# Trunk of a two-layer diffusion backbone: the first modulations by quarters of the features, one multiply for each value, and a new order of the start

## The chip, the cores and the metric

The kernel runs on one core of a Trainium2 chip. The metric is the time of one execution in microseconds (us), as the device measures it; the median of the runs is compared. The engines are PE (TensorE: matrix products; PEld is its weight load), DVE (VectorE), ACT (ScalarE), POOL (GpSimd) and SP (SyncE, which here only issues DMA loads). Each works through its own list of instructions, in the order of the code.

## The reference

Two layers over 256 latent tokens of 1024 features, with 256 context tokens ahead of the first. What the change touches is the head of layer 0:

```python
sh1, sc1, g1, sh2, sc2, g2 = jnp.split((c_s @ ada_w[i] + ada_b[i])[:, None, :], 6, axis=-1)
h = rmsnorm(x, norm1_g[i]) * (1 + sc1) + sh1
csh1, csc1, cg1, csh2, csc2, cg2 = jnp.split(cc_s @ ada_w[i] + ada_b[i], 6)
hc = rmsnorm(ctx, norm1_g[i]) * (1 + csc1) + csh1
q, k, v, f = jnp.split(h @ w_in, [DIFF_QK, 2 * DIFF_QK, 2 * DIFF_QK + DIFF_V], axis=-1)
kc, vc = jnp.split(hc @ w_in[:, DIFF_QK:2 * DIFF_QK + DIFF_V], [DIFF_QK], axis=-1)
```

`c_s` and `cc_s` are silu of the conditioning vectors of the tokens and of the context. After this come the attention with its six heads, a Fourier mixer, an output projection, an expert network with 16384 experts, a second layer of another kind with its own expert network, and a last norm.

## The kernel before

Features lie on partitions, tokens along the free axis: `x` and `xc` (context) are eight tiles of 128 features by 256 tokens. Products are made in fp32 out of parts: a value is split into a high part (a rounded copy, ACT) and a low part (the difference, DVE), and three products stand for one. Weights come in units of 128 x 1024 values (512 KB) through `Stream`: SP loads a unit into one of four buffers `raw`; `_split` makes `whi` on ACT (L109) and `wlo` on DVE (L111); the next load that gets the buffer waits until the split is done. Loads are issued in one order, so one that waits holds up those behind it.

The start of layer 0 is written out by hand in the string `START`; its words are run one after another, and each engine gets its instructions in that order:

- `M0` to `M15`: the 16 units of `ada_w` for shift and scale, a product of 2 or 4 rows with 512 columns each (`modulation`). M0 to M7 are used raw, in fp32 products (L547); M8 to M15 are split first (L555). Four units make one row of 512 columns.
- `sc`/`sx`, `ic`/`ix`, `rc`/`rx`: sum of squares, its inverse root (`ir`: DVE L269, then POOL L270), and its spread over all partitions (PE L277, ACT copy `rstd`), for context and for x.
- `C0`, `C1`: `columns` copies finished rows to SBUF (`ar`), turns them on PE into columns (L565), and makes shift `sh` and scale `sc` of a half of the features (L570 to L573).
- `nc0` to `nx7`: one normalisation each, on DVE (L596).
- `Dc0`, `Dx0`, `Dc1`, `Dx1`: `modulate`, for context (c) or x, a half of the features: scale and shift (ACT, `h`, L602), high part (ACT, L603: `chi` of context, `thi` of x) and low part (DVE, L604: `clo`, `tlo`).
- `Q` with three digits: a part of the value projection, of column chunk 0 to 2, token block 0 to 3 (0 and 1 context, 2 and 3 x) and half of the features: 12 products of 128 x 256 (L248 to L250). All chunks together are 288 products.
- `S`: split weights ahead; `a`: one step of another modulation, which DVE sums by itself (L445); `V`: the finished values leave PSUM.

The first product of the next part, the keys of head 0, is the first row `mm<-thi,whi` of L241. From there the six heads follow, with an order string of their own.

Of the kernel before, what the change touches and what calls it, by code (L numbers as in the profile page):

```python
# [20 lines left out]
P = 128  # L21
D = 1024
KT = 8
# [25 lines left out]
HL_BUFS = 3  # L49
MIX_BUFS = 6  # L50
# [7 lines left out]
START = "Lc Lx M0 sc M1 M2 M3 M4 M5 sx ic ix b S M6 S rc nc2 nc1 nc0 rx nc6 nx1 nx2 nc3 M7 nx0 nx3 C0 S nx4 M8 S Dc0 M9 S Dx0 Q000 M10 nx5 S Q010 M11 nc4 M12 Q020 nx7 S nc5 M13 Q030 M14 nc7 M15 nx6 C1 Q100 S Lk Q110 Dx1 Dc1 a Q120 S Q021 Q130 Q121 Q001 S Q101 Q111 a S Q031 a a Q011 V0 Q131 a Q220 S Q200 a a Q230 Q210 Q221 a S Q201 V1 a S Q231 S Q211 a V2".split()  # L58
# [5 lines left out]
class Stream:  # L64
# [4 lines left out]
    def __init__(self, nc, raw_pool, hl_pool):  # L69
        self.nc = nc  # L70
        self.raw_pool, self.hl_pools = raw_pool, [hl_pool, None]
# [16 lines left out]
    def load(self):  # L88
        while self.loaded < len(self.specs) and self.loaded < self.freed + RAW_BUFS:
            t = self.raw_pool.tile([P, 1024], F32, name="raw")  # L90
            self.nc.sync.dma_start(t, self.specs[self.loaded][0])
            self.raw[self.loaded] = t
            self.loaded += 1
# [49 lines left out]

    def next(self):
# [7 lines left out]
        self.cur = self.specs[n][2]  # L152
# [11 lines left out]
def trunk(ctx, tc, a, out):  # L164
# [344 lines left out]
    with ExitStack() as mx:  # L509
# [14 lines left out]
        with tc.tile_pool(name="m0n", bufs=2) as npl:  # L524
# [11 lines left out]
            rows = {}  # L536
# [57 lines left out]
            def normalize(j, k):  # L594
                dst, src, r = ((xn, x, st.get("x")), (xc, xc, st.get("c")))[j]
# [898 lines left out]
```

## Time and profile before

| | |
|---|---|
| median of 3 runs | 1973.15 us (1973.15 to 1973.7) |
| the profiled execution | 1970.44 us, of which its span 1968.7 |
| PE busy, share of the span | 98% |
| DVE, ACT busy | 80%, 48% |
| granted clock of PE, mean | 0.994 |
| from start to the first value product / the first key product | 30.09 / 77.67 us |

The profiled execution is one run; its times are taken from the span's first instruction. PE's busy share counts modelled ends of pipelined products, so a busy PE is not a PE at its peak. The granted clock is a share of 2.4 GHz.

### The profile page before, as it was taken

The numbers are of one execution on the slowest core, as the hardware profiler recorded it, in microseconds if no ns is written. First come the engines' busy times: TensorE is split into PE (matmuls) and PEld (weight loads), VectorE is DVE, ScalarE is ACT, GpSimd is POOL, SyncE is SP. The second block draws the span as 40 slices with busy tenths as digits, with TensorE's granted clock in tenths as the row PEclk, the third lists the DMA queues.
The fourth block names the chain that finished last, engine by engine and source line by source line (L and its number), as shares of the span: only waits on it lengthen the run. The fifth ranks groups of instructions, "written<-read, shape, count | busy, mean of one in ns | idle before, by whom it ended". The sixth has DMA issues, their size and how long they took to land. (4 is left out here: it accounts for less than half of the span.)

```text
span 1968.7 us, 35611 instructions
## 1 busy us (share of the span) xinstructions
PE 1924.6 (98%) x14172; PEld 1723.6 (88%) x14172; DVE 1567.0 (80%) x2972; ACT 939.1 (48%) x1493; POOL 11.6 (1%) x18
## 2 busy tenths in 40 slices
PE   7999999999999999999999899999999999999998
PEld 3977999999999877788888899999999987778886
DVE  5786779987887899998888678997777788885555
ACT  5445554444444444444445554445444444444544
POOL 0000000000000000000000000000000000000000
PEclk9999999999999999999999999999999999999999
DMA  7742556665666566678885365655555555556563
GB/s 266 266 165 82 159 175 185 186 184 188 199 184 185 186 208 206 210 253 284 280 280 186 132 186 172 187 184 183 171 165 168 169 169 173 165 173 196 178 191 119
DMA packets 106295, 374.03 MB, mean 190 GB/s; under 512 B 11920, under 2 KB 12560, under 8 KB 105744
## 3 DMA queue, kind: packets, MB, share of 16 engines
q1 hardware_dynamic: 104256, 366.23, 58.9%
q10 hardware_dynamic: 1872, 5.53, 0.9%
q8 instruction: 111, 1.82, 0.4%
q14 instruction: 56, 0.46, 0.1%
HBM read 370.66 MB, written 1.05 MB: 189 GB/s over the span
## 5 line engine op out<-in xcount | busy, mean ns | idle before, releaser
L111 DVE TENSOR_TENSOR wlo<-raw,whi 128x1024 fp32r<-128x1024 f32 x604 | 736.9, 1222 | 276.6 <-ACT whi L109 262.8
L109 ACT ACTIVATE whi<-raw 128x1024 fp32r<-128x1024 f32 x604 | 636.0, 1055 | 395.7 <-PE acc L1159 319.1
L241 PE MATMUL acc<-thi,whi 128*128 128x256 f32 (+1 forms) x2016 | 572.3, 285 | 0.0
L241 PE MATMUL acc<-thi,wlo 128*128 128x256 f32 (+1 forms) x2016 | 568.8, 283 | 0.4 <-DVE wlo L111 0.4
L241 PE MATMUL acc<-tlo,whi 128*128 128x256 f32 (+1 forms) x2016 | 559.8, 281 | 0.0
L241 PEld LDWEIGHTS acc<-thi,wlo 128*128 128x128 f32 x2016 | 382.9, 190 | 1.0 <-DVE wlo L111 0.8
L241 PEld LDWEIGHTS acc<-thi,whi 128*128 128x128 f32 x2016 | 382.1, 190 | 0.0
L241 PEld LDWEIGHTS acc<-tlo,whi 128*128 128x128 f32 x2016 | 376.4, 188 | 0.0
L1159 PE MATMUL acc<-whi,thi 128*128 128x512 f32 x1024 | 287.2, 400 | 0.0
L1159 PE MATMUL acc<-whi,tlo 128*128 128x512 f32 x1024 | 282.5, 396 | 0.2 <-DVE tlo L497 0.2
L1159 PE MATMUL acc<-wlo,thi 128*128 128x512 f32 x1024 | 282.2, 395 | 0.0
L1180 ACT ACTIVATE A<-acc 128x256 f32<-128x256 f32 x240 | 92.6, 386 | 391.5 <-PE acc L241 391.5
L1159 PEld LDWEIGHTS acc<-wlo,thi 128*128 128x128 f32 x1024 | 192.6, 188 | 47.5
L1159 PEld LDWEIGHTS acc<-whi,tlo 128*128 128x128 f32 x1024 | 192.6, 188 | 45.5 <-DVE tlo L497 0.6
L1159 PEld LDWEIGHTS acc<-whi,thi 128*128 128x128 f32 x1024 | 186.8, 188 | 38.9
L241 PE MATMUL mm<-thi,whi 128*128 128x256 f32 (+1 forms) x448 | 128.7, 287 | 0.9 <-ACT qp L1094 0.9
L241 PE MATMUL mm<-tlo,whi 128*128 128x256 f32 (+1 forms) x448 | 127.1, 284 | 2.4 <-DVE tlo L352 2.4
L241 PE MATMUL mm<-thi,wlo 128*128 128x256 f32 (+1 forms) x448 | 126.5, 282 | 0.0
L497 DVE TENSOR_TENSOR tlo<-A,thi 128x256 fp32r<-128x256 f32 x256 | 106.8, 418 | 0.0
L1144 DVE SCALAR_TENSOR_TENSOR A<-gg,A 128x512 f32<-128x512 f32 x128 | 87.6, 684 | 20.4 <-PE gg L1141 20.3
L496 ACT ACTIVATE thi<-A 128x256 fp32r<-128x256 f32 x256 | 102.5, 401 | 0.0
L1130 DVE TENSOR_TENSOR og<-o,gT 128x512 f16<-128x512 f16 x256 | 96.4, 417 | 0.1
(269 smaller groups left out, 1976.8 us busy)
## 6 DMA issues: line engine op xcount, KB each, us to landing
raw<-in_eu SPq DMA_DIRECT2D x256, 512.0 KB, 3.6
raw<-in_ev SPq DMA_DIRECT2D x256, 512.0 KB, 4.2
raw<-in_ada1t SPq DMA_DIRECT2D x56, 512.0 KB, 4.4
raw<-in_wq SPq DMA_DIRECT2D x32, 512.0 KB, 4.2
ada<-in_ada0t SPq DMA_DIRECT2D x48, 256.0 KB, 4.8
raw<-in_ada0h SPq DMA_DIRECT2D x16, 512.0 KB, 4.5
raw<-in_w_out SPq DMA_DIRECT2D x16, 512.0 KB, 3.7
raw<-in_o_in_u SPq DMA_DIRECT2D x8, 512.0 KB, 4.8
```

The source lines that it names most:

```text
L109: nc.scalar.activation(hi, r, AF.Copy)
L111: nc.vector.tensor_tensor(lo, r, hi.bitcast(F32), op=OP.subtract)
L241: nc.tensor.matmul(o, lhsT=w[:, k, :], rhs=t[:, k, :n], start=first and j == 0 and i == passes[0], stop=last and j == len(order) - 1 and i ...
L496: A_.activation(hi, src, AF.Copy)
L497: V.tensor_tensor(lo, src, hi.bitcast(F32), op=OP.subtract)
L1130: V.tensor_tensor(og[j], o1, of(gT[j], t0, 64), op=OP.mult)
L1144: return lambda: V.scalar_tensor_tensor(av, pt.rearrange("p t i -> p i t"), 1.0 / GSCALE, av, op0=OP.mult, op1=OP.mult)
L1159: nc.tensor.matmul(y[2 * h + tt], lhsT=w[a_][:, tt * P:tt * P + P], rhs=e[b_][:, 512 * h:512 * h + 512], start=i == 0 and n == 0, stop=i = ...
L1180: A_.activation(A[i // 64][:, i % 64, :], p[:, :T], AF.Gelu_apprx_tanh)
```

## The change

The rows of `ada_w` are laid out anew: a row of 512 columns is now shift and scale of one quarter of the features (two tiles of 128), so that four units give all that a quarter needs. `columns` is split in two: `A` copies the row (`row_out`), `C` turns it, with four products in place of eight transposes; for split rows a small matrix `pair` adds the two parts in the same product. There is no normalisation any more: `modulate` multiplies value, scale and inverse root in one DVE instruction (`t`, L613), ACT adds the shift and rounds (L615), and DVE makes the low part from `t` and the shift (L616). `Q`'s last digit now counts quarters, so that a `Q` has 6 products. The split units M8 to M15 have three buffers of their own. `S` is now exactly one split (`one`), and the words of `START` stand in a new order, in which context's quarter is modulated and multiplied while the units of later quarters are still to come. `START` holds 8 words `a` where it held 10; the heads take the steps that are left.

```diff
+ADA_BUFS = 3
...
-START = "Lc Lx M0 sc M1 M2 M3 M4 M5 sx ic ix b S M6 S rc nc2 nc1 nc0 rx nc6 nx1 nx2 nc3 M7 nx0 nx3 C0 S nx4 M8 S Dc0 M9 S Dx0 Q000 M10 nx5 S Q010 M11 nc4 M12 Q020 nx7 S nc5 M13 Q030 M14 nc7 M15 nx6 C1 Q100 S Lk Q110 Dx1 Dc1 a Q120 S Q021 Q130 Q121 Q001 S Q101 Q111 a S Q031 a a Q011 V0 Q131 a Q220 S Q200 a a Q230 Q210 Q221 a S Q201 V1 a S Q231 S Q211 a V2".split()
+START = "l1 Lc l4 M0 Lx b sc M1 M2 ic S M3 A0 rc C0 Dc0 Q000 Q010 M4 S Q100 Q110 sx M5 S ix M6 S rx Dx0 Q020 Q030 M7 A1 S Q120 Q130 M8 C1 Dc1 S Q001 Q011 M9 S Q101 Q111 Dx1 M10 S Q021 Q031 M11 A2 S Q121 Q131 S C2 Dc2 Q002 Q012 M12 S Q102 Q112 Dx2 M13 S Q022 Q032 M14 M15 A3 S Q122 Q132 C3 Dc3 Q003 Q013 Lk Q103 Q113 Dx3 Q023 Q033 S Q123 V0 Q133 a V1 Q200 Q210 a Q220 Q230 a Q201 Q211 S Q221 Q231 a Q202 S Q212 Q222 Q232 a a Q203 Q213 Q223 a Q233 a V2".split()
...
-    def load(self):
-        while self.loaded < len(self.specs) and self.loaded < self.freed + RAW_BUFS:
+    def load(self, n=RAW_BUFS):
+        while self.loaded < len(self.specs) and self.loaded < self.freed + n:
...
+    def one(self):
+
+        while self.specs[self.next_split][1] == "raw":
+            self.next_split += 1
+        n = self.next_split
+        self.load()
...
+        self._split(n)
+        self.next_split += 1
...
-            S.add(a["ada0h"][n:], 1, "raw" if n < 8 else "split")
-        if s[0] == "Q" and s[1::2] not in seen:
-            seen.add(s[1::2])
-            S.add(a["w_in_v"][2 * int(s[1]) + int(s[3]):], 1, "split")
+            S.add(a["ada0h"][n:], 1, "raw" if n < 8 else "split", 2 * (n >= 8))
+        if s[0] == "Q" and (s[1], int(s[3]) // 2) not in seen:
+            seen.add((s[1], int(s[3]) // 2))
+            S.add(a["w_in_v"][2 * int(s[1]) + int(s[3]) // 2:], 1, "split")
...
+    A_.dma_start(cols, a["cols"])
...
+    A_.dma_start(ident, a["consts"][:, K_ID:K_FOLD])
...
-            A_.dma_start(cols, a["cols"])
-            S.load()
-            A_.dma_start(ident, a["consts"][:, K_ID:K_FOLD])
-            sh = npl.tile([P, KT, 2], F32, name="sh", bufs=1)
-            sc = npl.tile([P, KT, 2], F32, name="sc", bufs=1)
+            ss = npl.tile([P, 2, KT, 2], F32, name="ss", bufs=1)
+            sh, sc = ss[:, 0], ss[:, 1]
             b2 = npl.tile([P, 16, 2], F32, name="b2", bufs=1)
-            xn = npl.tile([P, KT, T], F32, name="xn", bufs=1)
+            pair = npl.tile([4, 2], F32, name="pair", bufs=1)
...
-            def columns(half):
-                w = 2 + 2 * half
-                ar = npl.tile([4, 1024], F32, name="ar", bufs=1)
-                A_.activation(ar[:w, 0:512], rows[2 * half][0:w, :], AF.Copy)
-                A_.activation(ar[:w, 512:1024], rows[2 * half + 1][0:w, :], AF.Copy)
+            def row_out(c):
+                w = 2 if c < 2 else 4
+                ars[c] = npl.tile([4, 512], F32, name="ar")
+                A_.activation(ars[c][:w], rows.pop(c)[0:w, :], AF.Copy)
+
+            def columns(c):
+
+                w = 2 if c < 2 else 4
+                ar = ars.pop(c)
                 p = gb()
-                for n in range(8):
-                    nc.tensor.transpose(p[:, w * n:w * n + w], ar[:w, n * P:(n + 1) * P], ident[0:w, 0:w])
-                pv = p[:, :8 * w].rearrange("p (s c m) -> p s c m", s=2, m=w)
-                k = slice(4 * half, 4 * half + 4)
-                bias = b2.rearrange("p (s c) m -> p s c m", s=2)[:, :, k]
-                for i, o in enumerate((sh, sc)):
-                    V.tensor_tensor(o[:, k], pv[:, i, :, 0:2], bias[:, i], op=OP.add)
-                    if half:
-                        V.tensor_tensor(o[:, k], pv[:, i, :, 2:4], o[:, k], op=OP.add)
+                for n in range(4):
+                    nc.tensor.matmul(p[:, 2 * n:2 * n + 2], lhsT=ar[:w, n * P:(n + 1) * P],
+                                     rhs=ident[0:2, 0:2] if w == 2 else pair, start=True, stop=True)
+                k = slice(2 * c, 2 * c + 2)
+                V.tensor_tensor(ss[:, :, k], p[:, :8].rearrange("p (s c m) -> p s c m", s=2, m=2),
+                                b2.rearrange("p (s c) m -> p s c m", s=2)[:, :, k], op=OP.add)
                 V.scalar_tensor_tensor(sc[:, k], sc[:, k], 1.0,
-                                       ncol(C_NORM + 4 * half, 4)[:, :, None].to_broadcast([P, 4, 2]),
+                                       ncol(C_NORM + 2 * c, 2)[:, :, None].to_broadcast([P, 2, 2]),
                                        op0=OP.add, op1=OP.mult)
 
             def square_sums(src):
@@ -591,17 +606,14 @@
                 A_.activation(t, spread(r), AF.Copy)
                 return t
 
-            def normalize(j, k):
-                dst, src, r = ((xn, x, st.get("x")), (xc, xc, st.get("c")))[j]
-                V.tensor_tensor(dst[:, k, :], src[:, k, :], r, op=OP.mult)
-
-            def modulate(half, js):
-                for j, src, hi, lo in (((0, xn, thi, tlo), (1, xc, chi, clo))[js],):
-                    for k in range(4 * half, 4 * half + 4):
-                        h = npl.tile([P, T], F32, name="h", bufs=4)
-                        A_.activation(h, src[:, k, :], AF.Identity, scale=sc[:, k, j:j + 1], bias=sh[:, k, j:j + 1])
-                        A_.activation(hi[:, k, :T], h, AF.Copy)
-                        V.tensor_tensor(lo[:, k, :T], h, hi[:, k, :T].bitcast(F32), op=OP.subtract)
+            def modulate(c, j):
+                src, r, hi, lo = ((x, st.get("x"), thi, tlo), (xc, st.get("c"), chi, clo))[j]
+                for k in range(2 * c, 2 * c + 2):
+                    t = npl.tile([P, T], F32, name="t", bufs=4)
+                    V.scalar_tensor_tensor(t, src[:, k, :], sc[:, k, j:j + 1], r, op0=OP.mult, op1=OP.mult)
+                    b = sh[:, k, j:j + 1]
+                    A_.activation(hi[:, k, :T], t, AF.Identity, bias=b)
+                    V.scalar_tensor_tensor(lo[:, k, :T], t, b, hi[:, k, :T].bitcast(F32), op0=OP.add, op1=OP.subtract)
...
-            def quarter(outs, part, i, half):
-                for k in range(4 * half, 4 * half + 4):
+            def quarter(outs, part, i, c):
+                for k in range(2 * c, 2 * c + 2):
                     wide_part(outs[i], part, acts[i], k, k == 0 and i % 2 == 0, k == KT - 1 and i % 2 == 1)
...
                 elif c == "S":
-                    S.ahead()
+                    S.one()
+                elif c == "l":
+                    S.load(int(n))
...
                     V.tensor_copy(b2, ncol(C_ADAB, 16)[:, :, None].to_broadcast([P, 16, 2]))
+                    V.tensor_tensor(pair, ident[0:4, 0:2], ident[0:4, 2:4], op=OP.add)
...
-    w = f["ada_w"][0][:, :2048].reshape(4, 2, P, 2, 2, 512)
-    a["ada0h"] = np.ascontiguousarray(w.transpose(4, 3, 0, 2, 1, 5)).reshape(16, P, 1024)
+    w = f["ada_w"][0][:, :2048].reshape(4, 2, P, 2, 4, 256)
+    a["ada0h"] = np.ascontiguousarray(w.transpose(4, 0, 2, 1, 3, 5)).reshape(16, P, 1024)
```

How the order moves, at three places. PE, the beginning of the program (`mm<-raw,cs` are M units, `gg<-ones,sq` sums of squares, `gg<-ident,ir` the spread, `gg<-ident,ar` the turn). Before:

```order
L547 MATMUL mm<-raw,cs 2x512 x12
L264 MATMUL gg<-ones,sq 128x1 x4
L547 MATMUL mm<-raw,cs 2x512 x2
L277 MATMUL gg<-ident,ir 128x128 x4
L547 MATMUL mm<-raw,cs 2x512 x2
L565 MATMUL gg<-ident,ar 128x2 x8
L555 MATMUL mm<-whi,csr 4x512
```

and now:

```order
L561 MATMUL mm<-raw,cs 2x512 x6
L280 MATMUL gg<-ones,sq 128x1 x2
L561 MATMUL mm<-raw,cs 2x512 x2
L293 MATMUL gg<-ident,ir 128x128 x2
L583 MATMUL gg<-ident,ar 128x2 x4
L264 MATMUL acc<-whi,chi 128x256
```

The first value product (`acc<-whi,chi`) stands behind four M units and not behind ten; the sums and the spread of x have gone further down.

DVE, around the inverse roots (`raw_150` and `raw_154` are M8 and M9). Before:

```order
L269 TENSOR_SCALAR ir_164<-gg_161 128x2
L269 TENSOR_SCALAR ir_170<-gg_167 128x2
L648 COPY b2_118<-cols_71 128x32
L111 TENSOR_TENSOR wlo_175<-raw_150,whi_174 128x1024
L111 TENSOR_TENSOR wlo_179<-raw_154,whi_178 128x1024
```

and now, from the second value unit on (`raw_145`; `raw_208` and `raw_231` are M8 and M9, `ir_240` is x's):

```order
L112 TENSOR_TENSOR wlo_205<-raw_145,whi_204 128x1024
L596 TENSOR_TENSOR sq_224<-sq_224 128x1024
L596 TENSOR_TENSOR sq_224<-sq_224 128x512
L596 TENSOR_TENSOR sq_224<-sq_224 128x256
L112 TENSOR_TENSOR wlo_234<-raw_208,whi_233 128x1024
L285 TENSOR_SCALAR ir_240<-gg_237 128x2
L112 TENSOR_TENSOR wlo_248<-raw_231,whi_247 128x1024
L613 SCALAR_TENSOR_TENSOR t_256<-x_73,ss_111,rstd_251 128x256
L616 SCALAR_TENSOR_TENSOR tlo_85<-t_256,ss_111,thi_84 128x256
L613 SCALAR_TENSOR_TENSOR t_260<-x_73,ss_111,rstd_251 128x256
L616 SCALAR_TENSOR_TENSOR tlo_85<-t_260,ss_111,thi_84 128x256
```

The inverse root of x has moved from ahead of all splits to behind M8's, and the modulation is a chain that goes through ACT between each `t` and its low part.

ACT and DVE at the third quarter (`ar_398` is its row, `raw_290` a value unit, `raw_328` M13, `ss` shift and scale). ACT now:

```order
L575 ACTIVATE ar_398<-mm_304 4x512
L110 ACTIVATE whi_400<-raw_290 128x1024
L110 ACTIVATE whi_418<-raw_328 128x1024
L615 ACTIVATE chi_91<-t_431,ss_111 128x256
L615 ACTIVATE chi_91<-t_435,ss_111 128x256
```

DVE now:

```order
L112 TENSOR_TENSOR wlo_401<-raw_290,whi_400 128x1024
L112 TENSOR_TENSOR wlo_419<-raw_328,whi_418 128x1024
L586 TENSOR_TENSOR ss_111<-gg_424,b2_112 128x2x4
L588 SCALAR_TENSOR_TENSOR ss_111<-ss_111,cols_71 128x4
L613 SCALAR_TENSOR_TENSOR t_431<-xc_110,ss_111,rstd_165 128x256
```

and DVE before, at the second half's columns (`raw_305` is M15, `raw_311` a value unit):

```order
L111 TENSOR_TENSOR wlo_383<-raw_305,whi_382 128x1024
L111 TENSOR_TENSOR wlo_389<-raw_311,whi_388 128x1024
L596 TENSOR_TENSOR xn_119<-x_72,rstd_194 128x256
L570 TENSOR_TENSOR sh_116<-gg_402,b2_118 128x8
```

Two splits stand ahead of the scale in both, but before there was one such place, now there are three, the one after C3 with one split ahead.

## Rows read from the trace of the kernel before

**Rows 1.** The page, part 1: busy us of each engine (share of the span).

```profile
PE 1924.6 (98%) x14172; PEld 1723.6 (88%) x14172; DVE 1567.0 (80%) x2972; ACT 939.1 (48%) x1493; POOL 11.6 (1%) x18
```

**Rows 2.** Timeline of PE: start us, us, engine, line, operation [idle before <-releaser].

```profile
5.21 9.58 PE L547 MATMUL mm<-raw,cs 128*2 128x512 f32 x16 [5.21 <-ACT cs L233]
...
19.89 1.88 PE L547 MATMUL mm<-raw,cs 128*2 128x512 f32 x4
...
26.20 0.40 PE L555 MATMUL mm<-whi,csr 128*4 128x512 f32 x1
...
27.83 0.39 PE L555 MATMUL mm<-wlo,csr 128*4 128x512 f32 x1
30.09 0.38 PE L248 MATMUL acc<-whi,chi 128*128 128x256 f32 x1 [1.87 <-ACT chi L603]
...
50.10 0.28 PE L249 MATMUL acc<-wlo,chi 128*128 128x256 f32 x1
50.22 0.28 PE L250 MATMUL acc<-whi,clo 128*128 128x256 f32 x1
...
77.67 0.28 PE L241 MATMUL mm<-thi,whi 128*128 128x256 f32 x1
```

**Rows 3.** Windows of the start: us, busy us of each engine, granted clock, DMA share, GB/s.

```profile
28.00:32.00 4.00, 2.13 (x8) 1.37 (x7) 3.20 (x10) 2.92 (x7) 0.00 (x0) 0.86 0.72 235
32.00:36.00 4.00, 3.33 (x11) 1.83 (x11) 2.64 (x5) 3.90 (x8) 0.00 (x0) 0.50 0.27 105
36.00:38.00 2.00, 2.00 (x11) 1.90 (x10) 0.97 (x4) 1.94 (x5) 0.00 (x0) 0.58 0.87 262
40.00:77.67 37.67, 37.22 (x292) 33.75 (x291) 27.11 (x46) 20.80 (x36) 0.00 (x0) 1.00 0.85 288
```

**Rows 4.** Groups by line and form, 0 to 240 us: busy us, mean ns.

```profile
L111 DVE TENSOR_TENSOR wlo<-raw,whi 128x1024 fp32r<-128x1024 f32 x43 | 51.9, 1220 | 8.0 <-ACT whi L109 8.0
L109 ACT ACTIVATE whi<-raw 128x1024 fp32r<-128x1024 f32 x43 | 44.8, 1054 | 13.5 <-DMA raw<-in_ada0h 6.2 <-PE acc L250 4.6 <-DVE wlo L111 1.3
...
L371 DVE SCALAR_TENSOR_TENSOR nt<-x,sc,r 128x256 f32<-128x256 f32 x8 | 3.5, 482 | 2.8 <-ACT r L367 2.7
L352 DVE SCALAR_TENSOR_TENSOR tlo<-nt,mod,thi 128x256 fp32r<-128x256 f32 x8 | 3.5, 480 | 0.0
L351 ACT ACTIVATE thi<-nt,mod 128x256 fp32r<-128x256 f32 x8 | 3.4, 496 | 1.4 <-PE acc L241 1.4
```

**Rows 5.** Timelines of ACT and DVE, the modulation of context before.

```profile
29.62 0.42 ACT L603 ACTIVATE chi<-h 128x256 fp32r<-128x256 f32 x1
...
30.56 0.42 ACT L603 ACTIVATE chi<-h 128x256 fp32r<-128x256 f32 x1
...
31.95 0.42 DVE L604 TENSOR_TENSOR clo<-h,chi 128x256 fp32r<-128x256 f32 x1 [0.51 <-ACT chi L603]
```

**Rows 6.** Timelines: links of the chain from a row to its columns.

```profile
20.00 0.16 DVE L269 TENSOR_SCALAR ir<-gg 128x2 f32<-128x2 f32 x1 [0.29 <-PE gg L264]
...
19.80 1.36 POOL L270 TENSOR_TENSOR ir<-ir,mhalf 128x2 f32<-128x2 f32 x2 [19.35 <-DVE ir L269]
...
21.70 1.16 PE L277 MATMUL gg<-ident,ir 128*128 128x128 f32 x8
...
24.24 0.64 ACT L591 ACTIVATE rstd<-gg 128x256 f32<-128x256 f32 x2
24.77 0.57 ACT L561 ACTIVATE ar<-mm 2x512 f32<-2x512 f32 x1
...
25.39 0.88 PE L565 MATMUL gg<-ident,ar 2*128 2x2 f32 x8 [0.72 <-ACT ar L561]
```

**Rows 7.** DMA issues between 24 and 26 us: count, KB each, median us to landing.

```profile
raw<-in_ada0h SPq DMA_DIRECT2D x3, 512.0 KB, 4.4
```

**Rows 8.** One head: a window, and two of DVE's steps in its timeline.

```profile
111.00:128.00 17.00, 16.65 (x115) 14.32 (x113) 15.12 (x28) 8.77 (x20) 0.97 (x1) 1.00 0.57 207
...
113.39 1.53 DVE L445 SCALAR_TENSOR_TENSOR acca<-ada,cs,acca 128x512 f32<-128x512 f32 x2
```

More of the change, by code (lines that the diff above doesn't have):

```diff
@@ L70, in __init__ @@
         self.nc = nc
-        self.raw_pool, self.hl_pools = raw_pool, [hl_pool, None]
+        self.raw_pool, self.hl_pools = raw_pool, [hl_pool, None, None]
         self.specs = []
@@ L142, in _ahead @@
             self.next_split += 1
+    def one(self):
[3 more added lines that the diff above has]
+        self.load()
+        pool = self.specs[n][2]
+        assert n < self.loaded and self.specs[n][1] == "split"
+        assert sum(self.specs[i][2] == pool for i in self.hl) + (self.held if pool == 0 else 0) < (HL_BUFS, 0, ADA_BUFS)[pool]
+        self._split(n)
+        self.next_split += 1
     def next(self):
@@ L151, in next @@
         self.pos += 1
-        self.cur = self.specs[n][2]
+        if self.specs[n][2] < 2:
+            self.cur = self.specs[n][2]
         return self.hl.pop(n)
@@ L522, in trunk @@
         hg = big.tile([P, 1], F32, name="hg")
-        with tc.tile_pool(name="m0n", bufs=2) as npl:
+        with tc.tile_pool(name="m0n", bufs=2) as npl, tc.tile_pool(name="hla", bufs=ADA_BUFS) as hla:
+            S.hl_pools[2] = hla
             xc = npl.tile([P, KT, T], F32, name="xc", bufs=1)
-            A_.dma_start(cols, a["cols"])
-            S.load()
-            A_.dma_start(ident, a["consts"][:, K_ID:K_FOLD])
-            sh = npl.tile([P, KT, 2], F32, name="sh", bufs=1)
-            sc = npl.tile([P, KT, 2], F32, name="sc", bufs=1)
+            ss = npl.tile([P, 2, KT, 2], F32, name="ss", bufs=1)
+            sh, sc = ss[:, 0], ss[:, 1]
             b2 = npl.tile([P, 16, 2], F32, name="b2", bufs=1)
-            xn = npl.tile([P, KT, T], F32, name="xn", bufs=1)
+            pair = npl.tile([4, 2], F32, name="pair", bufs=1)
             csr = npl.tile([P, KT, 4], F32R, name="csr", bufs=1)
@@ L535, in trunk @@
             V.tensor_tensor(csr[:, :, 2:4], cs, csr[:, :, 0:2].bitcast(F32), op=OP.subtract)
-            rows = {}
+            rows, ars = {}, {}
             def modulation(n):
@@ L654, in trunk @@
                     st[n] = rstd(st[n])
-                elif c == "n":
-                    assert "r" + n[0] in done
-                    normalize(int(n[0] == "c"), int(n[1]))
+                elif c == "A":
+                    assert "M%d" % (4 * int(n) + 3) in done
+                    row_out(int(n))
                 elif c == "C":
-                    h = int(n)
-                    assert "b" in done and "M%d" % (8 * h + 7) in done
-                    columns(h)
+                    assert "b" in done
+                    columns(int(n))
                 elif c == "D":
-                    h, j = int(n[1]), n[0]
-                    assert "C%d" % h in done and all("n%s%d" % (j, k) in done for k in range(4 * h, 4 * h + 4))
-                    modulate(h, int(j == "c"))
+                    assert "C" + n[1] in done and "r" + n[0] in done
+                    modulate(int(n[1]), int(n[0] == "c"))
                 elif c == "Q":
@@ L671, in trunk @@
                         outs[cc] = banked([accb() for _ in range(2)])
-                    if (cc, h) not in parts:
-                        left[cc, h] = 4
+                    u = cc, h // 2
+                    if u not in parts:
+                        left[u] = 8
                         S.held = max(1, sum(v > 0 for v in left.values()))
-                        parts[cc, h] = S.next()
+                        parts[u] = S.next()
                     assert i % 2 == 0 or "Q%d%d%d" % (cc, i - 1, h) in done
-                    assert h == 0 or all("Q%d%d0" % (cc, q) in done for q in range(4))
-                    quarter(outs[cc], parts[cc, h], i, h)
-                    left[cc, h] -= 1
+                    assert h == 0 or "Q%d%d%d" % (cc, i, h - 1) in done
+                    quarter(outs[cc], parts[u], i, h)
+                    left[u] -= 1
                     S.held = max(1, sum(v > 0 for v in left.values()))
                 elif c == "V":
-                    assert all("Q%s%d1" % (n, q) in done for q in range(4))
+                    assert all("Q%s%d3" % (n, q) in done for q in range(4))
                     values_out(int(n), outs[int(n)])
```

## The prediction

> **What bounds the kernel now.** I read the page first: PE is busy for 98% of the span [rows 1]. That is a mean, and the change touches only the start, up to the first key product, so I then read that stretch in windows and as a timeline. PE does modulation rows from 5.21 us, has its first value product only at 30.09 us, and reaches the first key product at 77.67 us [rows 2]. From 40 us to there it is busy for 37.22 of 37.67 us; between 28 and 32 us it has only 2.13 of 4 [rows 3]. In that dip the granted clock falls: 0.86 of full from 28 to 32 us, 0.50 from 32 to 36 and 0.58 from 36 to 38, full again after 40 [rows 3]; 0.50 is the lower of the two levels, 1.2 GHz. So PE bounds the stretch from 40 us on, and what is to be won lies before it. After 77.67 us the order is the same in both kernels, so the change is worth what it moves that one moment by, plus what it hands on to the heads.
>
> **The prices.** In the dense part value products start 0.12 us apart (50.10, 50.22) and the eight products of two split modulation units 0.23 (26.20 to 27.83 for seven steps), so such a unit, four of them, costs 0.93 on PE. A raw unit (two fp32 products, four instructions) is 1.88 us to its modelled end at full clock (19.89), and some 1.72 from start to start, as the next work could begin before that end; the first four took 9.58 from 5.21 [rows 2]. A weight split is 1.05 us on ACT and then 1.22 on DVE [rows 4]. The old modulation keeps ACT's high parts 0.94 us apart, two ACT instructions for each feature, with DVE's low part beside it (31.95, idle 0.51 before it) [rows 5]. The new one has no row of its own; its three kinds of instruction stand later in the kernel: DVE multiply 0.48, ACT high part with a shift 0.50, DVE low part 0.48 [rows 4]. The code writes them feature by feature, multiply, low part, multiply, low part, so DVE waits for ACT inside each feature: 0.48 + 0.50 + 0.48, less the overlap of about 0.08 between neighbours and plus three hand-offs of some 0.03 (29.62 + 0.42 to 30.09 is 0.05 [rows 2, 5]), is 1.46 us. That is an estimate; its bounds are 0.94 (nothing waits) and 1.6 (no overlap). Sixteen of these take 23 us of DVE's time, where the old form had a normalisation and a low part of 0.42 each [rows 5], 13 in all.
>
> **The change part by part.** Times below are estimates, made by laying these rows along the after-order, engine by engine. M0 to M15 are the modulation units, Q the quarters of value products, C the turn of a row into columns.
>
> *The early start.* M0 to M3 run as they do now, 5.2 to 14.8, plus 0.5 for the context's sums in front of M3. Then row copy 0.57, turn about 0.8 (eight instructions at 25.39 have 0.1 each), scale 0.35 (two small DVE operations like the 0.16 at 20.00), multiply 0.48, high part 0.50 [rows 4, 6]: the first value product starts near 18.0, 12 us earlier than now.
>
> *The stall of x.* At the place shown for DVE, x's inverse root stands behind the split of M8. M8's load stands behind M7's on SP's queue, and M7's waits until PE has finished M4, near 22.6 (18.0, two products of context at 1.46 a feature, then M4's 1.72). Issued near 23.0 behind another, it lands 4.4 later as loads in a row do [rows 7]: 27.4. Split 1.05 + 1.22 ends near 29.8; inverse 0.16, power 0.70 (1.36 for two), spread 0.58, copy 0.38, multiply 0.48, high part 0.50, hand-offs 0.2 [rows 4, 6]: the first product of x starts at 32.7. PE ran out of other work near 27.9, after M6, and M7, whose weights are there, stands behind these products.
>
> *What is left at 32.7.* Of the 288 value products 24 are done: 264 x 0.119 = 31.4. M7 is 1.7, M8 to M15 8 x 0.93 = 7.4, three turns at 0.75 are 2.3: 42.8 us. At 30.09 the kernel before has M0 to M9 behind it and 34.3 + 6 x 0.93 + 0.9 = 40.8 left. So the new order is 4.6 us behind (75.5 against 70.9): x's stall has spent what the early start won, and more.
>
> *The turns.* Before, the second half has one turn, covered by products of the first half. Now each quarter has one, and a quarter's products are short: 48 x 0.119 = 5.7. After C1, scale 0.35, multiply, high part and hand-offs leave PE idle 1.5, then 1.1 between the two features: 2.6. After C2, ACT takes the row copy first, then a split (1.05), DVE that split and another (1.22 + 1.14) ahead of the scale, as the third order piece shows; that is 5.4 us from M11's end to the product, and PE has 1.43 of products and the turn to fill it: 3.2 idle, + 1.1 = 4.3. After C3 one split stands there: 2.0 + 1.1 = 3.1. The two first products of x wait 1.1 and 0.9. Sum 12.0. The first key product then comes at 32.7 + 42.8 + 12 = 87.5, **9.8 later than now**. Bounds: none of these waits, 75.5 (2.2 earlier than now); features at 1.6 instead of 1.46, +2.
>
> *The clock.* Before, a hole of 2 us in PE's work (27.83 + 0.39 to 30.09) came ahead of a stretch at half clock [rows 2], of (0.14 x 4 + 0.50 x 4 + 0.42 x 2) / 0.50 = 6.8 us [rows 3]. Then PE was waiting in much of it anyhow. Now the hole ahead of 32.7 is nearly 5 us with only the spread in it, and PE's work follows densely. I take one such stretch, half of its 6.8 us: **3.4**. Ends: 0 if the clock stays up; 6.8 more if the holes after C2 and C3 bring it down as well.
>
> The Trainium skill, "TensorE: Matmul & The Clock Gate", section "HAM oscillation — how this bites in real kernels", tells of kernels that let PE wait between bursts and pay the slow clock after each wait, not once. By that the holes behind C2 and C3 would count too, and the sum would be 6.8 larger; the trace of before agrees for its one hole, and shows no second.
>
> *The steps handed on.* START now holds 8 `a` steps, not 10, so the heads take two more of some 0.7 on DVE (1.53 for two at 113.39) [rows 8]. In a head DVE is busy 15.1 of 17 us, but PE is at 16.65 [rows 8]: between 0 and 1.4; neither engine has much room, so I take **0.7**.
>
> *The rest.* Dropping 16 normalisations and 16 ACT copies frees DVE and ACT of work that hides behind PE's 40 to 77 us: 0. Constants' earlier load, bias and pair: DVE and ACT's queue are idle then: 0. Ends of all these within 0.3.
>
> **Sum.** 9.8 + 3.4 + 0.7 = 13.9, on the profiled execution's 1970.44: 1984.3. That run lies 2.7 under the median of the runs, 1973.15, from which I forecast 1973.15 + 14 = **1987 us**.
>
> **The rivals.** *Faster:* the early products carry the stretch. From 18.0 PE has 288 x 0.119 + 4 x 1.72 + 7.4 + 2.3 + 1.1 for x's sums and spread = 52 us, which ends at 70; 7.7 earlier, 1965.5. It decides where PE's waits after 18.0 total under 7.7 us. For it: PE idles between 28.2 and 30.09 now, and loses clock there. Against: x's stall alone, 27.9 to 32.7, takes most of it. Chance 0.14. *No change:* waits of about 8, 1970 to 1976: 0.08. *More holes, more slow clock* (the mechanism of PE resting after every turn): 13.9 + 6.8 = 20.7, 1994. For it: three holes in place of one. Against: in slow stretches PE waits for DVE part of the time. Chance 0.20. *My forecast*, 1979 to 1991: 0.58.
>
> **How the numbers follow.** About 0.2% (4 us) is what a measurement of this kernel tells from no change. Slower is 0.58 + 0.20, faster 0.14, same 0.08. The range takes in the forecast's own 1979 to 1991, the slow clock up to 1996 and no change from 1970: what it leaves out is the faster case and a third of the case of more slow clock, together 2 in 10.
>
> **What would show it.** Right: first value product near 18, first product of x near 32 and after M8's split on DVE, holes on PE after the second and third turn, key product near 88 to 92, DVE alternating multiply and low part with 0.5 us idle inside each feature. Wrong: DVE doing the next feature's multiply inside that wait, M8's load landing before 25, the granted clock full throughout, or the key product before 78.

## The result, and the profile after

The changed kernel takes 2000.33 us (median of 4 runs, 2000.07 to 2000.54), the kernel before 1973.15 us in the same session: a ratio of 1.014, 95% interval 1.0128 to 1.0152, so 27.2 us slower. The direction was forecast; the amount was 14, and 1987 with a range to 1996 was too low. The profiled execution after has a span of 1998.3 us, that of before 1968.7. The one of before lies 2.7 us under its median and the one of after at its own, so the spans differ by 29.6 and the medians by 27.2. Of the 29.6 us, 22.3 lie ahead of the first key product, 6.1 in the six heads behind it and 1.2 in all the rest.

Part 1 of the page after, the line that answers to [rows 1]; PE does 19.6 us more by the modelled ends, though it has 16 instructions more and not one value product more:

```profile
PE 1944.2 (97%) x14188; PEld 1737.4 (87%) x14188; DVE 1570.7 (79%) x2973; ACT 931.8 (47%) x1477; POOL 12.9 (1%) x18
```

The timeline of PE after, which answers to [rows 2]: start us, us, engine, line, operation, and in brackets the idle time before it and what ended that.

```profile
19.04 0.39 PE L264 MATMUL acc<-whi,chi 128*128 128x256 f32 x1 [1.59 <-ACT chi L615]
...
22.81 2.46 PE L561 MATMUL mm<-raw,cs 128*2 128x512 f32 x4
...
33.46 0.71 PE L293 MATMUL gg<-ident,ir 128*128 128x128 f32 x4 [2.43 <-POOL ir L286]
35.70 0.58 PE L264 MATMUL acc<-whi,thi 128*128 128x256 f32 x1 [1.53 <-ACT thi L615]
...
47.17 0.38 PE L264 MATMUL acc<-whi,chi 128*128 128x256 f32 x1 [1.52 <-ACT chi L615]
...
48.63 0.58 PE L264 MATMUL acc<-whi,chi 128*128 128x256 f32 x1 [0.51 <-ACT chi L615]
...
63.72 0.38 PE L264 MATMUL acc<-whi,chi 128*128 128x256 f32 x1 [2.97 <-ACT chi L615]
...
78.75 0.58 PE L264 MATMUL acc<-whi,chi 128*128 128x256 f32 x1 [1.81 <-ACT chi L615]
...
99.96 0.28 PE L257 MATMUL mm<-thi,whi 128*128 128x256 f32 x1
```

The reader should see the early start, 19.04 us where it was 30.09 [rows 2], and then what it is spent on: the wait for x's inverse root (2.43, then 1.53 for its first feature) and a wait after each later turn (1.52, 2.97, 1.81). The first key product comes at 99.96, 22.3 us later than before.

Windows of the start after, which answer to [rows 3]: us, busy us of PE, PEld, DVE, ACT, POOL, granted clock, DMA share, GB/s.

```profile
16.00:20.00 4.00, 2.33 (x15) 1.73 (x14) 1.69 (x5) 1.10 (x4) 0.00 (x0) 1.00 0.91 313
20.00:24.00 4.00, 3.51 (x11) 2.22 (x12) 2.49 (x3) 3.19 (x3) 0.00 (x0) 0.57 0.20 83
...
36.00:40.00 4.00, 3.65 (x13) 2.64 (x13) 1.04 (x3) 0.51 (x1) 0.00 (x0) 0.50 0.45 139
...
48.00:52.00 4.00, 3.49 (x13) 2.45 (x13) 2.96 (x5) 2.40 (x3) 0.00 (x0) 0.50 0.04 6
...
60.00:64.00 4.00, 1.03 (x9) 0.95 (x8) 3.35 (x6) 1.38 (x2) 0.00 (x0) 1.00 0.43 128
64.00:68.00 4.00, 3.44 (x14) 2.52 (x14) 2.68 (x5) 1.71 (x3) 0.00 (x0) 0.62 0.41 136
...
80.00:84.00 4.00, 3.80 (x17) 3.78 (x18) 2.25 (x5) 1.17 (x3) 0.00 (x0) 0.50 0.91 320
...
5.20:99.96 94.76, 79.78 (x400) 54.60 (x399) 45.98 (x76) 33.53 (x51) 2.42 (x2) 0.86 0.61 204
```

The same window of the kernel before, from PE's first row to its first key product:

```profile
5.20:77.67 72.47, 67.17 (x385) 45.17 (x386) 45.86 (x83) 39.66 (x65) 1.36 (x2) 0.95 0.81 282
```

These two rows hold the account of the 22.3 us. PE sits idle for 94.76 - 79.78 = 15.0 us and not 72.47 - 67.17 = 5.3: 9.7 more. The clock that was not granted, the window times one less the granted clock, is 0.14 x 94.76 = 13.3 us and not 0.05 x 72.47 = 3.6: another 9.7 (the clock stands to two digits, so this is good to half a us; idle time inside a slow stretch is counted in both parts, some 1.5 us by windows of 2 us). Ahead of the first key product, where there was one stretch at half clock (1.2 GHz), there are five, near 20, 36, 48, 64 and 80 us, and each comes behind one of the waits above. What is left, 2.9 us (4.4 if the doubly counted 1.5 is taken off), is for the larger part the turns: the groups of PE by line have 4.2 us for the four turns where the kernel before has 1.6 for two (0.88 for the first, [rows 6]):

```profile
L264 PE MATMUL acc<-whi,chi 128*128 128x256 f32 x48 | 17.6, 367 | 10.1 <-ACT chi L615 9.8 <-ACT vt L631 0.3
...
L583 PE MATMUL gg<-ident,ar 2*128 2x2 f32 x16 | 2.1, 249 | 0.0
L583 PE MATMUL gg<-pair,ar 4*128 4x2 f32 x16 | 2.1, 249 | 0.0
```

The first of these groups also names whom PE waits for: 9.8 of its 15 idle us end with a high part of context.

DVE after, around context's first modulation and x's inverse root; it answers to [rows 5] and [rows 6]:

```profile
17.96 0.48 DVE L613 SCALAR_TENSOR_TENSOR t<-xc,ss,rstd 128x256 f32<-128x256 f32 x1
19.02 0.48 DVE L616 SCALAR_TENSOR_TENSOR clo<-t,ss,chi 128x256 fp32r<-128x256 f32 x1 [0.57 <-ACT chi L615]
19.42 0.48 DVE L613 SCALAR_TENSOR_TENSOR t<-xc,ss,rstd 128x256 f32<-128x256 f32 x1
20.47 0.48 DVE L616 SCALAR_TENSOR_TENSOR clo<-t,ss,chi 128x256 fp32r<-128x256 f32 x1 [0.57 <-ACT chi L615]
...
31.33 1.22 DVE L112 TENSOR_TENSOR wlo<-raw,whi 128x1024 fp32r<-128x1024 f32 x1 [5.70 <-ACT whi L110]
32.47 0.15 DVE L285 TENSOR_SCALAR ir<-gg 128x2 f32<-128x2 f32 x1
```

Features are 19.42 - 17.96 = 1.46 us apart, as estimated. The inverse root of x runs right behind M8's split, which had kept DVE waiting for 5.70 us; the sums for it had left PE by 29.2. ACT shows that M8's load was what that split waited for:

```profile
30.24 1.06 ACT L110 ACTIVATE whi<-raw 128x1024 fp32r<-128x1024 f32 x1 [7.05 <-DMA raw<-in_ada0h]
```

Behind the first key product the order is the same but for the two steps handed on, and the heads take longer. Their stretch, up to the first product of the output projection that waits for its weights' low part, as a window after, and ahead of it the last head's scores on PE:

```profile
99.96:234.00 134.04, 126.06 (x797) 105.40 (x795) 102.72 (x196) 66.82 (x144) 5.62 (x6) 0.92 0.41 137
```

```profile
197.75 3.42 PE L742 MATMUL acc<-kh,qh 64*128 64x512 f32 x6 [2.52 <-DVE qh L731]
```

The same two lines before:

```profile
77.67:205.57 127.90, 119.47 (x796) 101.11 (x794) 99.26 (x187) 67.31 (x146) 5.30 (x6) 0.99 0.41 136
```

```profile
172.49 1.95 PE L728 MATMUL acc<-kh,qh 64*128 64x512 f32 x6 [1.08 <-DVE qh L717]
```

The idle time hardly differs (8.0 now, 8.4 before); the clock does. Ahead of the last head's scores the heads now take 97.79 us (99.96 to 197.75) where they took 94.82, and from there to the end of the stretch 36.25 (to 234.00, at 0.91 of full clock) where they took 33.08 (at 1.00).

### The profile page after: what moved, and what is told of

It reads as the page before. It is cut to its first block, busy times and chain, and to the rows that moved or that the text cites. A ratio compares the mean times of both kernels' runs of the same rounds, so it can differ in the third digit from the quotient of the medians.

```text
span 1998.3 us, 35624 instructions
## 1 busy us (share of the span) xinstructions
PE 1944.2 (97%) x14188; PEld 1737.4 (87%) x14188; DVE 1570.7 (79%) x2973; ACT 931.8 (47%) x1477; POOL 12.9 (1%) x18
## 3 DMA queue, kind: packets, MB, share of 16 engines
HBM read 370.66 MB, written 1.05 MB: 186 GB/s over the span
```

## The experiments

All times are medians, against runs of the kernel before on the same chip. The columns behind the first are read from the profiled executions: "start" is the window from 5.20 us to the first key product, "heads" the stretch just shown. The 95% intervals given below with the ratios reach some 3 us to either side (2 for e7, e9, e10 and e12), so a gain that is the difference of two medians is known to no better than that.

| kernel | above before, us | first key product | PE idle, start | clock, start | heads, us | clock, heads |
|---|---|---|---|---|---|---|
| before | | 77.67 | 5.3 | 0.95 | 127.90 | 0.99 |
| changed | 27.2 | 99.96 | 15.0 | 0.86 | 134.04 | 0.92 |
| e1, x ahead | 20.7 | 93.57 | 11.8 | 0.88 | 132.87 | 0.96 |
| e2, turns ahead | 22.6 | 95.67 | 10.9 | 0.89 | 135.74 | 0.91 |
| e3, both multiplies first | 19.7 | 92.84 | 12.5 | 0.88 | 131.43 | 0.96 |
| e4, form only | 11.1 | 88.36 | 9.4 | 0.86 | 130.27 | 0.96 |
| e5, e1 to e3 together | 9.0 | 85.63 | 7.4 | 0.96 | 131.18 | 0.96 |
| e6, unread products | 21.2 | 94.61 | 6.0 | 0.98 | 132.07 | 0.96 |
| e7, form, multiplies ahead | 1.6 | 80.13 | 6.9 | 0.95 | 129.20 | 0.97 |
| e8, ten steps | 22.2 | 100.16 | 14.8 | 0.86 | 129.68 | 0.97 |
| e9, before with eight steps | 2.1 | 76.88 | 5.5 | 0.95 | 130.55 | 0.96 |
| e10, before with unread products | 0.9 | 76.60 | 3.5 | 0.98 | 129.19 | 0.97 |
| e11, e5 with both | 7.7 | 84.00 | 4.7 | 0.96 | 130.01 | 0.96 |
| e12, before with twelve steps | -0.5 | 76.73 | 4.4 | 0.95 | 128.52 | 0.97 |

### Three waits, each by itself: e1, e2, e3

e1 moves the words of x:

```diff
-Dc0 Q000 Q010 M4 S Q100 Q110 sx M5 S ix M6 S rx Dx0 Q020 Q030
+Dc0 sx Q000 Q010 M4 ix S Q100 Q110 rx Dx0 M5 S M6 S Q020 Q030
```

> The changed kernel, but x's sums, inverse root, spread and first modulation stand ahead of the splits of M8 and M9. If x's stall behind M8's split is a main cause, the wait of 2.43 us before the spread and most of the 1.5 us before x's first product go, one stretch of slow clock with them, and the time falls by 4 to 7 us, to 1993 to 1996. Rival, the weights' loads pace the start anyhow: the same waits turn up later in front of M8 to M11, and it stays within 1.5 us of 2000.3.

1993.45 us, ratio 1.0105 (1.0088 to 1.0122): 20.7 above before, a gain of 6.5 on the change. Neither the spread nor x's first product waits any more; the spread starts at 28.06 and x's first product runs without idle time ahead of it, behind M5 and M6:

```profile
28.06 0.61 PE L293 MATMUL gg<-ident,ir 128*128 128x128 f32 x4
28.59 3.60 PE L561 MATMUL mm<-raw,cs 128*2 128x512 f32 x8
32.12 0.39 PE L264 MATMUL acc<-whi,thi 128*128 128x256 f32 x1
```

The theory holds in the main. PE's idle time falls by 3.2 us and not by the 4.0 of the two waits, because a new one of 1.18 us turns up at 26.64, for the low part of a value weight that DVE now makes behind x's sums. The rival, that the loads pace the start anyhow, falls: none of the same waits comes back ahead of M8 to M11.

e2 moves the turns and the splits behind them (the second quarter's edit; the third and fourth have the same):

```diff
-A1 S Q120 Q130 M8 C1 Dc1 S
+A1 S Q120 C1 Dc1 Q130 M8 S
```

> The changed kernel, but in the second to fourth quarter the turn and context's modulation stand ahead of the splits, and one value product (12 in a row) covers the chain. If the splits ahead of the scale and the short cover make the holes after the turns (1.52, 2.97 and 1.81 us), these fall to under 1.5 us together and up to three stretches of slow clock go: 5 to 12 us faster, 1988 to 1995. Rival, the holes come from the chain through DVE and ACT alone whatever stands ahead: under 2.5 us faster.

1995.41 us, ratio 1.0113 (1.0096 to 1.0130): a gain of 4.6, between the two theories' numbers. The waits after the turns fell from 6.3 together to 1.7, near the 1.5 that the first theory has:

```profile
45.98 0.39 PE L264 MATMUL acc<-whi,chi 128*128 128x256 f32 x1 [0.50 <-ACT chi L615]
...
58.95 0.39 PE L264 MATMUL acc<-whi,chi 128*128 128x256 f32 x1 [0.61 <-ACT chi L615]
...
73.99 0.39 PE L264 MATMUL acc<-whi,chi 128*128 128x256 f32 x1 [0.60 <-ACT chi L615]
```

The slow stretches did not all go with the long waits. The one behind the first of these turns is gone (1.00 from 44 to 56 us); behind the other two the clock still falls, to 0.66 from 60 to 64 us and 0.50 from 76 to 80, after two waits of 0.55 to 0.61 us each, before the first and the second feature. That fits a gain under the forecast 5 to 12. The heads, at 0.91 of full clock, gave 1.7 us of it back in the profiled run.

e3 writes both multiplies of a quarter ahead of both low parts:

```diff
+                ts = {}
                 for k in range(2 * c, 2 * c + 2):
                     t = npl.tile([P, T], F32, name="t", bufs=4)
...
+                    ts[k] = t
+                for k, t in ts.items():
                     b = sh[:, k, j:j + 1]
```

> The changed kernel, but both multiplies of a quarter stand on DVE ahead of both low parts. If the wait for ACT inside each feature matters, the seven waits of 0.35 to 0.55 us before the second feature's product go: 2 to 4 us faster, 1996 to 1998. Rival, it hides behind what is late elsewhere: within 1 us of 2000.3.

1992.46 us, ratio 1.0101 (1.0084 to 1.0118): a gain of 7.5, twice what the theory asked for, from the smallest edit of the three (its profiled execution lies 2.8 us under its median). DVE now spends 0.18 us waiting for a pair of features instead of 0.57 for each, and the low parts of both are out 1.95 us after the first multiply's start, which was 2.99 (17.96 to 20.47 + 0.48):

```profile
17.22 0.88 DVE L614 SCALAR_TENSOR_TENSOR t<-xc,ss,rstd 128x256 f32<-128x256 f32 x2
18.28 0.89 DVE L619 SCALAR_TENSOR_TENSOR clo<-t,ss,chi 128x256 fp32r<-128x256 f32 x2 [0.18 <-ACT chi L615]
```

Visible idle time fell by 2.5 only; the rest of the gain is products that stood closer together, and clock.

### The three together: e5

> The changed kernel with the edits of e1, e2 and e3 together. If the three (x ahead of the splits, the turns ahead of the splits, both multiplies first) take away different waits, their gains of 6.9, 4.9 and 7.9 us add up in part: 1980 to 1985. Rival, each gain is the same slow clock escaped, so that they don't add: 1988 to 1993.

1981.51 us, ratio 1.0047 (1.0030 to 1.0064). The gains add up: 6.5 + 4.6 + 7.5 = 18.6 expected, 18.2 measured. In the start alone, by the column of the first key product, they add up less well: 6.4 + 4.3 + 7.1 = 17.8 against 14.3. So they are in the main three causes and not one clock seen three times, though the close match of the medians is in part chance. The granted clock of the start is 0.96 here, where each edit alone left it at 0.88 or 0.89:

```profile
5.20:85.63 80.43, 73.00 (x401) 47.44 (x401) 45.35 (x76) 32.70 (x51) 3.40 (x2) 0.96 0.69 240
```

### The form of the modulation: e4 and e7

e4 is the kernel before, halves and order unchanged, with the new modulation alone (and so without the normalisations):

```diff
-                        A_.activation(h, src[:, k, :], AF.Identity, scale=sc[:, k, j:j + 1], bias=sh[:, k, j:j + 1])
-                        A_.activation(hi[:, k, :T], h, AF.Copy)
-                        V.tensor_tensor(lo[:, k, :T], h, hi[:, k, :T].bitcast(F32), op=OP.subtract)
+                        V.scalar_tensor_tensor(t, src[:, k, :], sc[:, k, j:j + 1], st["xc"[j]], op0=OP.mult, op1=OP.mult)
+                        A_.activation(hi[:, k, :T], t, AF.Identity, bias=b)
+                        V.scalar_tensor_tensor(lo[:, k, :T], t, b, hi[:, k, :T].bitcast(F32), op0=OP.add, op1=OP.subtract)
```

> The kernel before, halves and order as they were, without its normalisations and with the one-multiply modulation in place of scale, shift and copy. If the form is no cause, it stays within 2 us of 1973.2 (the first value product some 0.5 later or earlier, the features 1.46 apart instead of 0.94 but behind other work). Rival, the form itself costs, because each low part waits for ACT behind its multiply: 4 us slower or more, a sixth of the loss or more.

1983.89 us, ratio 1.0054 (1.0037 to 1.0071): 11.1 slower, so the rival holds. Its windows show the price twice over, as idle time of PE and as 18 us at about half clock:

```profile
30.00:36.00 6.00, 4.07 (x12) 2.58 (x13) 3.81 (x8) 2.47 (x4) 0.00 (x0) 0.56 0.29 108
36.00:48.00 12.00, 9.08 (x31) 5.69 (x32) 7.70 (x12) 6.04 (x8) 0.00 (x0) 0.51 0.41 127
```

e7 is e4 with each multiply written ahead of the low part of the feature before it, so that DVE has a multiply to do while ACT makes the high part:

```diff
-                    for k in range(4 * half, 4 * half + 4):
-                        ...
+                    for k in ks:
+                        ...
+                        if k > ks[0]:
+                            low(k - 1)
+                    low(ks[-1])
```

> The kernel before with the one-multiply modulation as in e4, but each multiply written ahead of the low part of the feature before it. If e4 lost its 11 us because a multiply waits behind a low part that waits for ScalarE, features come about 1 us apart again and most of it returns: 1973 to 1977. Rival, the work that the form puts on VectorE itself is what costs: 1980 to 1984.

1974.11 us, ratio 1.0007 (0.9997 to 1.0016): nearly all returns, by the order of the same instructions; the interval takes in no difference from the kernel before. On DVE a multiply and a low part now follow each other at 0.40 us, 0.80 for a feature instead of the 1.46 of e4 (29.78 - 28.33 for its first two multiplies is 1.45):

```profile
29.31 0.49 DVE L602 SCALAR_TENSOR_TENSOR clo<-t,sh,chi 128x256 fp32r<-128x256 f32 x1 [0.18 <-ACT chi L607]
29.71 0.48 DVE L606 SCALAR_TENSOR_TENSOR t<-xc,sc,rstd 128x256 f32<-128x256 f32 x1
30.11 0.48 DVE L602 SCALAR_TENSOR_TENSOR clo<-t,sh,chi 128x256 fp32r<-128x256 f32 x1
```

### The clock by itself: e6, e10

e6 leaves the changed kernel's work and order alone and adds products that nobody reads ahead of the waits (the expectation says 70; the numbers that it lists, and the kernel, make 80):

```diff
+                elif c == "F":
+                    p = gb()
+                    ...
+                    for _ in range(int(n)):
+                        nc.tensor.matmul(p[:, :T], lhsT=lh, rhs=rh, start=True, stop=True)
```

> The changed kernel with 70 products that nobody reads, put on TensorE ahead of the waits after the first turn, ahead of and behind x's spread, and after the later turns (12, 16, 10, 10, 20 and 12 of 128x128 by 128x256): all other work and waits are as in the changed kernel. If the slow clock is what the holes cost beyond their own length, the granted clock stays up in the start and the first key product comes 5 to 12 us earlier: 1988 to 1995. Rival, the chains of waits pace the start and the clock hides behind them: the products fill holes and nothing moves, 1998 to 2003.

1993.71 us, ratio 1.0108 (1.0091 to 1.0125): with 80 products more to do the kernel is 6.0 us faster than the changed one, and its first key product comes 5.4 earlier. Two of the windows that stood at 0.57 and 0.50 above are at full clock, a third is better than it was:

```profile
20.00:24.00 4.00, 3.75 (x16) 1.85 (x17) 2.74 (x3) 2.94 (x3) 0.00 (x0) 1.00 0.13 53
36.00:40.00 4.00, 3.93 (x12) 1.58 (x13) 0.48 (x1) 0.00 (x1) 0.00 (x0) 0.67 0.23 95
48.00:52.00 4.00, 3.98 (x28) 2.99 (x27) 2.96 (x5) 1.98 (x3) 0.00 (x0) 1.00 0.29 67
```

So the slow clock costs time beyond the waits themselves. The 5.4 us are a lower bound of its share in the start, since the unread products can overrun a wait and one stretch is still slow.

e10 puts 12 such products ahead of the first value product of the kernel before.

> The kernel before with 12 products that nobody reads, on TensorE ahead of the first value product, where it waits 1.87 us. If the slow clock that follows that wait costs its full 3.4 us, 1969 to 1971. Rival, TensorE waits for context's features in that stretch at either clock: within 1 us of before.

1973.51 us, ratio 1.0006 (0.9997 to 1.0015): no gain. The start did get 1.1 us shorter at a clock of 0.98, but the heads, untouched, took 129.19 us at 0.97 and not 127.90 at 0.99.

### The steps handed on: e8, e9, e12

e8 is the changed kernel with two more words `a` at the end of the start, ten in all.

> The changed kernel with 10 steps a in the start, as before, instead of 8. By the forecast two steps cost the heads 0.7 us: 1999.6, and the stretch after the first key product stays some 6 us longer than before. Rival, the two steps make the heads late and bring the slow clock there: that stretch loses its 7 us, 1993 to 1996.

1994.68 us, ratio 1.0119 (1.0102 to 1.0136): 22.2 above before, 5.0 less than the change. The first key product did not move (100.16); the gain is in the heads, where the last head's scores wait 1.07 us and no longer 2.52:

```profile
100.16:229.84 129.68, 120.98 (x796) 102.44 (x794) 101.78 (x195) 66.50 (x144) 5.29 (x6) 0.97 0.41 140
```

```profile
196.74 1.52 PE L742 MATMUL acc<-kh,qh 64*128 64x512 f32 x5 [1.07 <-DVE qh L731]
```

The rival holds for five of its seven us, and the rows show where. The heads as a whole are 4.36 us shorter. The scores start 1.21 us sooner after the first key product (96.58 for 97.79), and from there to the end of the stretch it is 33.10 us at full clock and not 36.25 at 0.91: 3.15 us are the slow clock behind the longer wait. The other kernels agree. In the four whose last scores wait 2.5 us (the changed one, e1, e2, e6) this last part takes 36.25 to 37.77 us; in the ten that wait 0.3 to 1.6 us it takes 33.08 to 33.10. The number of steps alone does not make that wait: e3, e5 and e9 have eight steps too and wait 0.94 or 0.95, and in them a slow stretch stands some way ahead of these scores, which would keep PE back as well.

e9 takes two steps from the start of the kernel before, e12 adds two.

> The kernel before with 8 steps a in the start instead of 10. If the two steps that the change hands on are what makes its heads late (two more of 0.75 us ahead of the last head's query, and the slow clock behind the longer wait), the stretch after the first key product grows by 1.5 to 5 us: 1974 to 1977.5. Rival, they hide, and the changed kernel's late heads come from its other timing alone: within 1 us of before.

> The kernel before with 12 steps a in the start instead of 10. If steps in the last head cost as e9 is to show, two fewer there give back 1 to 2 us: 1970.5 to 1972. Rival, the start's steps wait for their loads and hold up splits of weights behind them: 1973 to 1976.

e9: 1974.71 us, ratio 1.0013 (1.0004 to 1.0022), 2.1 slower. The size fits the theory, its mechanism does not: the last head waits 0.94 us for its query and not longer than before, but the heads run at 0.96: their scores come 97.46 us after the first key product and not 94.82, with a slow stretch ahead of them (0.50 from 84 to 88 us after the first key product), and the part behind takes the same 33.09. e12: 1972.10 us, ratio 1.0001 (0.9992 to 1.0010), no difference; the expected gain did not come, nor the loss.

### What is left: e11

e11 is e5 with ten steps and with 12 unread products each after the first and second turn.

> The kernel of e5 with 10 steps a in the start and 12 unread products each after the first and the second turn. If the rest of e5's loss (9 us) is two stretches of slow clock and the steps, it adds up: 3.4 from the clock, 2 to 5 from the heads, 1973 to 1976. Rival, what is left is waits for weights and features: 1979 to 1981.

1980.35 us, ratio 1.0035 (1.0021 to 1.0049): 1.3 better than e5 by the table, and the rival's number. Its row of the start:

```profile
5.20:84.00 78.80, 74.10 (x424) 51.33 (x423) 46.12 (x77) 32.67 (x50) 2.32 (x2) 0.96 0.72 249
```

PE is idle for 4.7 us, less than before, at about the clock of before, and still reaches the key product 6.3 us later: with the 24 unread products (some 2.9 us at 0.12) and the turns (2.6 more than before) that leaves about 0.8. The unread products stand where PE would wait, so the chains seem to hold it up still, only not idly (no run separates this), and the turns are work that the halves did not have; the early start has not made up for these two. No version here is faster than the kernel before by more than the measurement is uncertain.

## Why the prediction was wrong in size

The direction and the places of the waits were right. Two terms of the sum were far too small, the slow clock and the steps handed on, and the rival with more slow clock was the nearer forecast, though it too was 6 us short.

**The early start.** Forecast 18.0 us, measured 19.04. The turn took 1.05 and not 0.8, and had to wait for the spread of context that stands ahead of it on PE; the hand-offs between engines were left out.

**The stall of x.** Forecast: inverse root behind M8's split, first product of x at 32.7. Measured: in that order, at 35.70; e1 shows it to be worth 6.5 us of the whole. The 3.0 us came ahead of the step "M7's waits until PE has finished M4, near 22.6": M4 ended at 25.27, and M8's load was issued and landed 2.7 to 2.8 later by it. Of that 1.0 is the late first product and some 1.6 came with the clock, which was already down by then (0.57 from 20 to 24): from the first value product to the end of M4 it took 6.2 us in place of 4.6, with M4 at 2.46 and not 1.88. The forecast had the first slow stretch only behind x's stall.

**The turns.** Forecast for what comes behind the first product of x: 10.0 us of waiting after the three turns and 2.0 for x's features; measured as idle after the turns 1.52 + 0.51, 2.97 + 0.55 and 1.81 + 0.35, 7.7 together, and 0.35 for x's features. So these waits were taken 4 us too long. The order behind them was right: e2 takes the long ones away and gains 4.6. Only the second of these turns has two splits ahead of its scale; ahead of the first there is one, and DVE was waiting for the turn itself there (0.74 us, to 45.69).

**Without the clock** the first key product was forecast at 87.5. Measured: 99.96 less the 13.3 us of clock not granted, 86.7 (some 88.5 if idle time in slow stretches isn't counted as clock). The match is in part luck: waits 4 us too long made up for a product of x that came 3.0 late.

**The clock.** This is the first step that failed: "I take one such stretch, half of its 6.8 us: 3.4". There are five stretches, and 13.3 us of clock were not granted in place of 3.4: 9.9 too few. (Against before, whose own 3.6 lie inside its 77.67, it is the 9.7 above.) e6 confirms at least 5.4 us of it. The reason given against the rival, that in slow stretches PE waits for DVE part of the time, does not hold: from 80 to 84 us PE is busy for 3.80 of 4 us at 0.50, and for 3.44 to 3.65 in the other slow windows above. That rival had three stretches and 10.2. The Trainium skill, "TensorE: Matmul & The Clock Gate", section "HAM oscillation — how this bites in real kernels", tells of a kernel that waits for DMA between bursts of products and pays the slow clock after each wait, not once. In the start the trace agrees, with five slow stretches behind five waits; in the heads not every wait has one, as is said below.

The prediction also says of holes with a slow clock behind them that the trace of before "shows no second". It shows one, in the heads, behind waits of 0.41, 0.89 and 0.89 us within three us; the granted clock is 0.50 from 106 to 109 us, and 0.90 in a window of 17 us around it:

```profile
103.69 0.66 PE L760 MATMUL acc<-ident,aa 128*128 128x128 f32 x4 [0.89 <-DVE aa L752]
105.24 3.14 PE L728 MATMUL acc<-kh,qh 64*128 64x512 f32 x8 [0.89 <-DVE qh L717]
```

```profile
94.70:111.70 17.00, 14.81 (x96) 11.94 (x96) 15.12 (x28) 8.03 (x17) 0.00 (x0) 0.90 0.50 174
```

Reading these lines first would have spoken for a slow stretch behind every turn.

**The steps handed on.** "Between 0 and 1.4 ... I take 0.7" is the other failed step: e8 puts it at 5.0, e9, in the other order, at 2.1. The bound counted DVE's work alone. The heads had 0.99 of the clock to lose: with two steps of 0.75 more the last head's scores wait 2.52 us for their query and not 1.07, and behind that wait alone the slow clock costs 3.15 of the 4.36 us that the heads of e8 are shorter by.

**The sum.** In the profiled executions the forecast was 13.9 above before and 29.6 came, 15.7 more: 9.9 of clock in the start, less 0.8 for the rest of it (86.7 for 87.5), 5.4 in the heads (6.1 for 0.7) and 1.2 behind the heads, which the forecast had at nothing. In medians the miss is 13.3; the 2.4 between is mostly that the profiled execution of before lies 2.7 under its median.

**What the forecast left unpriced.** "The code writes them feature by feature, so DVE waits for ACT" was seen and sized rightly at 1.46, but as a property of the change and never set against the same instructions in another order. e3 gains 7.5 and e7 9.5 us (11.1 to 1.6) by that order alone. Also the ceiling: before, PE had 5.3 us idle and 3.6 of clock not granted ahead of its first key product, so that no order of the same work could win more than about 8.9 there. The faster rival's 7.7 asked for nearly all of it.

**Still open** is which waits bring the slow clock. The heads of all kernels have waits, mostly of 0.3 to 1.1 us, at the same few places, and the clock falls behind one to three of them: once in before, e7, e8, e10 and e12, three times in the changed kernel and e2 (the last of these behind the 2.5 us), twice in the others. That is where their clocks of 0.99 to 0.91 come from. Equal waits differ: in before, 0.86 and 0.69 us (at 138.84 and 140.63) leave the clock at full; in e8, 0.87 and 0.69 at the same place of the heads (161.84 and 163.62) are followed by 6 us at 0.50. These are single profiled executions, so they can't tell the kernel's part in this from the run's. e8 and e9 put the steps' price at 5.0 and 2.1, with intervals that leave either open by some us.

## What to carry to other kernels

When the bound engine is busy for nearly all of a stretch, add up first what it has to lose there, idle time and clock not granted: an earlier start can win no more than that, and here more, shorter stages added a wait each. Price a wait of TensorE with the slow clock that may follow it, for every wait and not once, and ask the same of stages that merely follow. Each of the five long waits in the start of the changed kernel, and each wait of 2.5 us in the heads of four kernels, had a slow stretch behind it; of the shorter ones some had and some had not, so that such a price is a range. A value that goes from one engine through another and back should have the next value's first instruction written ahead of its last: that one order was worth 7.5 us (e3) and 9.5 us (e7) here, at least as much as any move of a stage (6.5 and 4.6).

## What was not expected of the hardware

Work that nobody reads made the kernel faster: 80 products more, 6.0 us less, because the granted clock of the start went from 0.86 to 0.98. And the clock of a later stretch, whose order had not changed, fell with changes ahead of it (0.99 to 0.92 in the heads), which undid gains of 1 to 2 us in e2 and e10.
